# A planner without filler matmuls in a recurrent scan, and two block products laid four abreast

## The chip, the cores and the metric

The program runs on one core of one Trainium2 chip. The metric is the time of one execution on the device in microseconds (us); of the kernel before, three runs gave a median of 3036.94 us (3034.74 to 3039.24).

## What is computed

The model is a two-layer backbone of width 1024 over 1024 latent tokens, with 256 context tokens ahead of them. Layer 0 mixes tokens by a recurrence with 16 heads of 64 channels, once forwards and once backwards; layer 1 mixes by a Fourier transform; behind each stands a squared-ReLU MLP of hidden width 4096. Cut to what matters here:

```python
w_log = -softplus(-(w0[d] + tanh(xw @ w1[d]) @ w2[d])) - 0.5          # rates of the recurrence, per direction
decay = exp(-exp(w_log)); iclr = sigmoid(a0[d] + (xa @ a1[d]) @ a2[d])
k_d = k * (1 + (iclr - 1) * ka); a, b = -kk, kk * iclr                 # kk is k, normalised per head
def step(s, inp):                                                      # one token; s is (head, 64, 64)
    w_t, k_t, v_t, a_t, b_t = inp[:5]
    sa = einsum('bhvk,bhk->bhv', s, a_t)
    s = s * w_t[:, :, None, :] + sa[..., None] * b_t[:, :, None, :] + v_t[..., None] * k_t[:, :, None, :]
    y = einsum('bhvk,bhk->bhv', s, inp[5])
    return s, y
for d in range(2):                                                     # forwards and backwards
    yc, s_ctx = scan(context tokens, s0, reverse=d == 1)
    yl, _ = scan(latent tokens, s_ctx, reverse=d == 1)
x = x + ga1 * (readout(yl of both directions) @ wo)
x = x + ga2 * mlp(modulate(rmsnorm(x)))                                # layer 0
x = x + ga1 * (real(fft2 of modulate(rmsnorm(x))) @ ft_wo)             # layer 1
x = x + ga2 * mlp(modulate(rmsnorm(x)))
return rmsnorm(x) * final_g
```

All of it is in 32-bit floating point.

## The kernel before, in words

The program has four stages. The first computes the norms, the projections and the factors of the recurrence and writes these factors to HBM. The second is the scan. The third reads the scan's output back and runs the readout, and the last, the longest, is the MLP, the Fourier layer and the second MLP.

**The scan** treats 64 tokens (a chunk) at a time, so there are 20 steps: 4 over the context and 16 over the latent tokens. A step works on one chunk of each direction, d = 0 and d = 1, for 16 heads in pairs: a tile has heads on its partitions 0 to 63 and 64 to 127 (hh = 0 and 1) and 8 such pairs along its free axis (q, or y = 8 d + q over both directions). The matmuls of a step, with the line at which the profile books them, are:

- L951 (`mms`): products of the factors inside a chunk, four bursts of 8 matmuls. ScalarE (L960, L964) and VectorE (L967, L972) take them out of PSUM.
- L1130 (`turn`): transposes of the factors, two bursts.
- The inverse of a 64x64 triangular matrix per head and direction, `scan_invert`. The 64 rows are two blocks of 32. VectorE inverts the 16x16 diagonal blocks by a long series of small operations (L1071 to L1117), L1141 and L1154 (each two bursts of 32 matmuls) finish the two 32x32 diagonal blocks, and the block off the diagonal is a product of three: L1173 (`v_mm`), then a copy to SBUF, then L1184 (`g_mm`), then a copy into the inverse `tt`.
- L1008 (`x_mm`), L1017 (`u_mm`, which multiplies by `tt`) and L1031 (`s_mm`): the recurrence itself, each once per direction. The state of step i enters `x_mm` of step i + 1. L1047 and L1053 (`r_mm`, `y_mm`) make the output of latent steps.

The off-diagonal block joins the first half of a chunk with the second. The partitions are four groups of 32 (g = 0 to 3), and both directions keep the first half in groups 0 and 2 and the second in 1 and 3. So `v_mm` reads group 0 and writes group 1, or reads 2 and writes 3, alternating for 16 values of y; `g_mm` goes back the other way.

**The order of the work** is made by a planner (`Plan`). Every operation is added with its engine, a planned length in us and the data that it needs; `emit` then simulates all engines by these lengths, picks at each turn the operation that can start first (of equals the one with the longest chain behind it), and writes the program in that order. Each engine runs its queue in that order, so an operation whose inputs come late holds up all behind it on its engine. The planner also models TensorE's clock: time is cut in windows of 3.413 us (`TICK`), and work in a window is planned at half speed where the one before had too little of it; each operation has a `load`, the weight with which its time counts.

**Fills.** Where the planner sees TensorE idle ahead of an operation that opens a new PSUM bank, it writes dummy 128x128 matmuls of the identity into that bank, one per 0.218 us of the gap (`FILL`). They are L1843 in the profile. They stand in TensorE's queue like any other work.

The trace has two rows for each matmul of the scan (a 32-bit matmul is done in two passes) and as many weight loads; the transposes of L1130 have one.

## Time and profile before

| | |
|---|---|
| median of three runs | 3036.94 us |
| the profiled execution: its time, its span | 3052.24 us, 3050.2 us |
| its granted TensorE clock, mean | 0.947 |
| TensorE busy over the span | 2858.6 us, 94% |
| VectorE, ScalarE, GpSimd busy | 1880.4, 1014.3, 487.8 us |
| first and last L1843 rows of the scan in the trace | at 659.13 and 1254.96 us |

A profile's engines are PE (TensorE's matmuls), PEld (its weight loads), DVE (VectorE), ACT (ScalarE), POOL (GpSimd) and SP (the queue of the sync engine, which issues DMAs). A row of a group of instructions gives line, engine, operation, output<-input, the count after x, then busy us, mean ns of one, and the idle time of the engine just before them with what ended it. "issue" is time in which the engine waited for nothing that the profile shows.

### The profile page before, as it was taken

The numbers are of one execution on the slowest core, as the hardware profiler recorded it, in microseconds if no ns is written. First come the engines' busy times: TensorE is split into PE (matmuls) and PEld (weight loads), VectorE is DVE, ScalarE is ACT, GpSimd is POOL, SyncE is SP. The second block draws the span as 40 slices with busy tenths as digits, with TensorE's granted clock in tenths as the row PEclk, the third lists the DMA queues.
The fourth block names the chain that finished last, engine by engine and source line by source line (L and its number), as shares of the span: only waits on it lengthen the run. The fifth ranks groups of instructions, "written<-read, shape, count | busy, mean of one in ns | idle before, by whom it ended". The sixth has DMA issues, their size and how long they took to land.

```text
span 3050.2 us, 63412 instructions
## 1 busy us (share of the span) xinstructions
PE 2858.6 (94%) x26844; PEld 2225.1 (73%) x26844; DVE 1880.4 (62%) x3363; ACT 1014.3 (33%) x1974; POOL 487.8 (16%) x415
## 2 busy tenths in 40 slices
PE   9999989988887888799999999999899999999998
PEld 5443446467777777688788888887798788888887
DVE  5398695546667666787655665454876554454455
ACT  4263454345555555333212111112322111111121
POOL 2063453300000000111110111010421110111110
PEclk9999999968789897799999999999899999999999
DMA  9266475623345443643222322211121111111111
GB/s 280 83 180 185 129 195 172 181 83 101 113 125 154 124 124 120 205 132 97 90 86 90 111 90 90 63 62 34 47 76 42 56 49 49 42 56 49 35 45 56
DMA packets 297293, 312.90 MB, mean 103 GB/s; under 512 B 81025, under 2 KB 212225, under 8 KB 297009
## 3 DMA queue, kind: packets, MB, share of 16 engines
q1 hardware_dynamic: 295648, 304.01, 33.3%
q8 instruction: 210, 3.44, 0.5%
q0 software_dynamic: 1360, 4.84, 0.5%
q14 instruction: 75, 0.61, 0.1%
HBM read 246.38 MB, written 62.39 MB: 101 GB/s over the span
## 4 chain that ended last, share of the span: by engine, by line
PE 78%; DVE 10%; DMA 4%; issue 4%; ACT 3%; SPq 1%; POOL 1%; DVEq 0%; ACTq 0%; POOLq 0%
PE ps L368 17%; PE ps L370 17%; PE ps L369 17%; PE ps L624 6%; PE ps L621 4%; PE ps L951 3%; PE ps L1843 2%; DVE bU L460 1%; PE ps L1008 1%; PE ps L1031 1%; PE ps L1017 1%; PE ps L1154 1%; PE ps L578 1%; PE ps L1053 1%; PE ps L1141 1%
## 5 line engine op out<-in xcount | busy, mean ns | idle before, releaser
L368 PE MATMUL ps<-rU,rU 128*128 128x512 f32 (+3 forms) x2632 | 980.1, 372 | 16.8 <-DVE rX L1538 8.0
L370 PE MATMUL ps<-rU,rU 128*128 128x512 f32 (+3 forms) x2632 | 976.1, 371 | 6.2 <-DVE rU L1268 3.5
L369 PE MATMUL ps<-rU,rU 128*128 128x512 f32 (+3 forms) x2632 | 975.9, 371 | 0.1
L368 PEld LDWEIGHTS ps<-rU,rU 128*128 128x128 f32 x2632 | 501.5, 191 | 111.9 <-DVE rX L1538 8.9
L370 PEld LDWEIGHTS ps<-rU,rU 128*128 128x128 f32 x2632 | 501.5, 191 | 97.8 <-DVE rU L1268 4.8
L369 PEld LDWEIGHTS ps<-rU,rU 128*128 128x128 f32 x2632 | 501.9, 191 | 90.3 <-DVE rU L1352 0.4
L1538 DVE SCALAR_TENSOR_TENSOR rX<-ps,mods,rX 128x512 f32<-128x512 f32 (+1 forms) x528 | 375.6, 729 | 123.8 <-PE ps L370 121.7
L1517 ACT ACTIVATE rS<-ps 128x512 f32<-128x512 f32 x122 | 73.0, 598 | 681.5 <-PE ps L370 680.8
L1268 POOL TENSOR_TENSOR rU<-rW,rU 128x512 fp32r<-128x512 f32 x73 | 118.0, 1621 | 1001.6 <-PE ps L370 518.3
L624 PE MATMUL ps<-bU,bU 128*128 128x512 f32 (+1 forms) x544 | 235.1, 568 | 2.6 <-ACT bS L427 1.9
L427 ACT CAST rU<-rW 128x512 fp32r<-128x512 f32 x161 | 97.2, 617 | 349.0 <-PE ps L370 260.9
L1268 DVE TENSOR_TENSOR rU<-rW,rU 128x512 fp32r<-128x512 f32 x201 | 173.3, 881 | 25.4 <-ACT rU L427 25.3
L427 DVE CAST rU<-rS 128x512 fp32r<-128x512 f32 (+1 forms) x97 | 45.0, 469 | 232.8 <-ACT rS L1520 205.4
L427 DVE CAST rU<-rW 128x512 fp32r<-128x512 f32 x115 | 55.1, 491 | 212.6 <-PE ps L369 210.3
L624 PEld LDWEIGHTS ps<-bU,bU 128*128 128x128 f32 x544 | 99.5, 191 | 108.2 <-issue 96.3
L621 PE MATMUL ps<-bU,bU 128*128 128x512 f32 x304 | 140.9, 604 | 0.0
L951 PE MATMUL ps<-sU,sX 64*128 64x128 f32 (+1 forms) x1280 | 119.3, 338 | 17.5 <-DVE sU L967 5.9
L951 PEld LDWEIGHTS ps<-sU,sX 64*128 64x128 f32 x1280 | 105.7, 241 | 24.7 <-issue 6.6
L427 ACT COPY sU<-ps 32x512 f32<-32x512 f32 (+1 forms) x167 | 96.2, 577 | 79.6 <-PE ps L1154 27.6
L967 DVE TENSOR_TENSOR sU<-ps,sW 64x256 f32<-64x256 f32 x160 | 67.5, 422 | 70.7 <-ACT sX L960 39.1
L1268 POOL TENSOR_TENSOR rU<-rS,rU 128x512 fp32r<-128x512 f32 x41 | 64.1, 1566 | 289.8 <-ACT rU L427 154.8
L1843 PE MATMUL ps<-ident 128*128 128x128 f32 x664 | 98.9, 308 | 2.8 <-DMA ident<-in_k_ident_dram 2.6
(275 smaller groups left out, 3740.8 us busy)
## 6 DMA issues: line engine op xcount, KB each, us to landing
rW<-in_mlp_w_dram SPq DMA_DIRECT2D x256, 256.0 KB
rW<-in_k_mwt_dram SPq DMA_DIRECT2D x96, 256.0 KB
sX<-s_bk SPq DMA_DIRECT2D x40, 512.0 KB
s_ar<-bU SPq DMA_DIRECT2D x32, 512.0 KB
sU<-s_ar SPq DMA_DIRECT2D x64, 256.0 KB
sW<-in_k_mwt_dram SPq DMA_DIRECT2D x64, 256.0 KB
bU<-in_rk_wk_dram SPq DMA_DIRECT2D x48, 256.0 KB
bU<-in_rk_wv_dram SPq DMA_DIRECT2D x48, 256.0 KB
```

Of the source, the lines that this page charges most:

```text
L368: nc.tensor.matmul(out, w[0], x[0], start=start, stop=False)
L369: nc.tensor.matmul(out, w[0], x[1], start=False, stop=False)
L370: nc.tensor.matmul(out, w[1], x[0], start=False, stop=stop)
L427: self.nc.scalar.copy(out, src) if e == "act" else self.engines[e].tensor_copy(out, src)
L621: fn = lambda B=B, x=x, w=w, ms=ms, kt=kt: nc.tensor.matmul(B.tile, x[:, ms], w, start=kt == 0, stop=kt == KT - 1)
L624: fn = lambda B=B, x=x, w=w, ms=ms, kt=kt, n=n: nc.tensor.matmul(B.tile[:, :n], w[:, ms], x[:, :n], start=kt == 0, stop=kt == KT - 1)
L951: nc.tensor.matmul(BB[hh].tile[:, j * P : j * P + nr], bk[HR[hh], q, :], L[hh][HR[hh], q, :nr], start=True, stop=True)
L967: plan.add("dve", 0.41, lambda bv=bv, ro=ro, hh=hh, q4=q4, d=d, L=L: nc.vector.tensor_tensor(L[hh][ro, q4, 0:C], bv()[ro, :, 0:C], self.ma ...
L1268: plan.flex({"dve": n / 960 + 0.07, "pool": n / 440 + 0.08}, lambda e: self.engines[e].tensor_tensor(out(1), src(), f32(out(0)), ALU.subtr ...
L1517: plan.flex({"act": 0.53, "dve": 0.6}, lambda e, B=B, s=s: nc.scalar.activation(s.tile[:, :512], B.tile, AF.Relu) if e == "act" else nc.ve ...
L1538: plan.add("dve", n / 960 + 0.12, lambda B=B, m=m, n=n, xs=xs: nc.vector.scalar_tensor_tensor(xs(), B.tile[:, :n], self.mod(layer, 5, m), ...
L1843: self.plan.fill = lambda t: nc.tensor.matmul(t[:, :P], self.ident, self.ident, start=True, stop=True)
```

## The change

There are three parts.

**No fills from scan step 4 on.** A flag `bare` on an operation stops the planner from writing fills ahead of it. It is set for steps 4 to 19 and cleared for what comes after the scan.

**Planned lengths.** The planned lengths of the scan's matmul bursts are set to other values: most grow (0.95 to 1.1 or 1.15 us), `turn` shrinks (0.85 to 0.75). Nothing but the planner reads them, so they show only as another order.

**Halves swapped in direction 1.** For d = 1, the two 32-token halves of a chunk trade places on the partitions: two of the factor products of the first stage write their result with the halves exchanged (`hv(...)[:, :, flip]`), the masks are rolled by 32 accordingly, and the zero blocks of `tt` and the copies into `mab` follow. The first half of d = 0 then lies in groups 0 and 2, that of d = 1 in groups 1 and 3. `v_mm` now takes for each of 8 values of q four products, 0 to 1, 1 to 0, 2 to 3 and 3 to 2, all four groups at a time. The number of matmuls is the same, 32 in each burst. The result of `v_mm` has 128 partitions and 256 columns and is copied at once, where two copies of 32 partitions and 512 columns stood; that of `g_mm` is copied by four copies of 32x256 in place of two of 32x512. `g_mm` now needs all four copies of the diagonal blocks.

```diff
-        self.step, self.rank = None, 0.0
+        self.step, self.rank, self.bare = None, 0.0, False
...
-                  hold=hold, dear=self.dear, weigh=self.weigh)
+                  hold=hold, dear=self.dear, weigh=self.weigh, bare=self.bare)
...
             if e == "pe" and blank:
-                fills = max(0, int((start - since - self.SLACK) / self.FILL))
+                fills = 0 if op["bare"] else max(0, int((start - since - self.SLACK) / self.FILL))
                 for _ in range(fills):
                     since = self.clock(since, self.FILL, 1.0)
                 start = max(start, since)
...
-        self.flex_tt(n, bk[:, :ng, 0], gv(ta), p1[:, :ng], ALU.mult, [kta, kp1], [(kbk, 0)])
+
+        hv = lambda ap: ap.rearrange("p g (w t) -> p g w t", w=2)
+        self.flex_tt(n, hv(bk[:, :ng, 0])[:, :, flip], hv(gv(ta)), hv(p1[:, :ng]), ALU.mult, [kta, kp1], [(kbk, 0)])
         self.flex_tt(n, bk[:, :ng, 1, flip], gv(kd), p1[:, :ng], ALU.mult, [kkd, kp1], [(kbk, 1)])
-        self.flex_tt(n, ar[:, :ng, 0], gr(kk), p0[:, :ng, 0:C], ALU.mult, [kkk, kp0], [(kar, 0)])
+        self.flex_tt(n, hv(ar[:, :ng, 0])[:, :, flip], hv(gr(kk)), hv(p0[:, :ng, 0:C]), ALU.mult, [kkk, kp0], [(kar, 0)])
...
-            for g in (1, 3):
-                plan.add("pool", 0.6, lambda tt=tt, g=g: nc.gpsimd.memset(tt[32 * g : 32 * g + 32, :, 0:32], 0.0), (), [(("tt", j), g)])
+            for g in range(4):
+                d = 1 - g % 2
+                plan.add("pool", 0.4, lambda tt=tt, g=g, d=d: nc.gpsimd.memset(
+                    tt[32 * g : 32 * g + 32, 8 * d : 8 * d + 8, 32 * d : 32 * d + 32], 0.0), (), [(("tt", j), g)])
...
         for i in range(NCH):
             self.plan.step = i
+            self.plan.bare = i >= 4
             self.scan_step(i)
...
-        RZ = [[slice(hh * 64 + 32 * z, hh * 64 + 32 * z + 32) for hh in range(2)] for z in range(2)]
+
+        RZ = [[[slice(hh * 64 + 32 * (d ^ z), hh * 64 + 32 * (d ^ z) + 32) for hh in range(2)] for d in range(2)] for z in range(2)]
...
-                plan.add("pe", 0.95, mms, [kb, (kL, "a", 0), (kL, "a", 1)],
+                plan.add("pe", 1.15, mms, [kb, (kL, "a", 0), (kL, "a", 1)],
...
                     plan.add("act", 0.38, lambda B=B, hh=hh, ys=ys, d=d: nc.scalar.activation(
-                        mab[RZ[0][hh], :, ys].rearrange("p w q t -> p q w t"),
-                        B.tile[RZ[0][hh]].rearrange("p (q w t) -> p q w t", q=4, w=4)[:, :, 0:2], AF.Copy, scale=-0.5),
+                        mab[RZ[0][d][hh], :, ys].rearrange("p w q t -> p q w t"),
+                        B.tile[RZ[0][d][hh]].rearrange("p (q w t) -> p q w t", q=4, w=4)[:, :, (slice(0, 2), slice(1, None, -1))[d]], AF.Copy, scale=-0.5),
                         [B], [(kM, d, hh, h4, 0)], B)
                     plan.add("act", 0.28, lambda bv=bv, hh=hh, ys=ys, d=d: nc.scalar.activation(
-                        mab[RZ[1][hh], 0, ys], bv()[RZ[1][hh], :, 32:C], AF.Copy, scale=-0.5),
+                        mab[RZ[1][d][hh], 0, ys], bv()[RZ[1][d][hh], :, 32 - 32 * d : C - 32 * d], AF.Copy, scale=-0.5),
...
-            self.at = plan.add("pe", 0.95, x_mm, lall + vall, [B], B, load=0.95)
+            self.at = plan.add("pe", 1.1, x_mm, lall + vall, [B], B, load=0.95)
...
-            plan.add("pe", 0.95, u_mm, [kx, *kT], [U], U, load=0.5)
+            plan.add("pe", 1.1, u_mm, [kx, *kT], [U], U, load=0.5)
...
-                plan.add("pe", 1.1, s_mm, vall + [(kt_, 0), (kt_, 1)], [B, kt0], B, load=0.78)
+                plan.add("pe", 1.2, s_mm, vall + [(kt_, 0), (kt_, 1)], [B, kt0], B, load=0.78)
...
-                plan.add("pe", 0.95, r_mm, vall + [E["ks"], (kL, "a", 0), (kL, "a", 1)], [Y], Y, load=0.5)
-                plan.add("pe", 1.05, y_mm, vall + [(k2, hh, h4) for hh in range(2) for h4 in range(2)], [Y], Y, load=1.0)
+                plan.add("pe", 1.15, r_mm, vall + [E["ks"], (kL, "a", 0), (kL, "a", 1)], [Y], Y, load=0.5)
+                plan.add("pe", 1.15, y_mm, vall + [(k2, hh, h4) for hh in range(2) for h4 in range(2)], [Y], Y, load=1.0)
...
-            plan.add("pe", 0.85, turn, [S[d]["kb"]], [*TB[d]], load=0.5)
+            plan.add("pe", 0.75, turn, [S[d]["kb"]], [*TB[d]], load=0.5)
...
-            plan.add("pe", 0.7, lambda w=w: h_mm(w), [kxt, *ms], [(H, w)], load=0.15)
+            plan.add("pe", 0.85, lambda w=w: h_mm(w), [kxt, *ms], [(H, w)], load=0.15)
...
-            plan.add("pe", 0.75, lambda w=w: t_mm(w), [khp, kxd], [(T, w)], load=0.3)
+            plan.add("pe", 0.85, lambda w=w: t_mm(w), [khp, kxd], [(T, w)], load=0.3)
...
+
+        four = [(d, 2 * hh + d, 2 * hh + 1 - d) for hh in range(2) for d in range(2)]
+        own = lambda g: slice(32 * (g % 2), 32 * (g % 2) + 32)
+
         def v_mm():
-            for y in range(16):
-                for g in (0, 2):
-                    nc.tensor.matmul(V.tile[Q[g + 1], y * 32 : y * 32 + 32], mab[Q[g], 1, y, :], tr[Q[g], y, :], start=True, stop=True)
-
-        plan.add("pe", 0.75, v_mm, [ktr, *offs], [V], V, load=0.15)
+            for q in range(8):
+                for d, f, l in four:
+                    nc.tensor.matmul(V.tile[Q[l], q * 32 : q * 32 + 32], mab[Q[f], 1, 8 * d + q, :], tr[Q[f], 8 * d + q, :], start=True, stop=True)
+
+        plan.add("pe", 0.65, v_mm, [ktr, *offs], [V], V, load=0.25)
         vt, kvt = slot("vt")
-        for g in (1, 3):
-            plan.flex({"act": 0.58, "dve": 0.69}, lambda e, g=g: self.copy_on(e, vt[Q[g]].rearrange("p y t -> p (y t)"), V.tile[Q[g]]),
-                      [V], [(kvt, g)], V)
+        plan.flex({"act": 0.38, "dve": 0.42}, lambda e: self.copy_on(e, vt.rearrange("p q t -> p (q t)"), V.tile[:, :256]), [V], [kvt], V)
 
         def g_mm():
-            for y in range(16):
-                for g in (1, 3):
-                    nc.tensor.matmul(G.tile[Q[g - 1], y * 32 : y * 32 + 32], vt[Q[g], y, :], tt[Q[g], y, 32:64], start=True, stop=True)
-
-        plan.add("pe", 0.75, g_mm, [(kvt, 1), (kvt, 3), (kT, 1), (kT, 3)], [G], G, load=0.15)
-        for g in (0, 2):
-            plan.flex({"act": 0.58, "dve": 0.69}, lambda e, g=g: self.copy_on(
-                e, tt[Q[g], :, 32:64], G.tile[Q[g]].rearrange("p (y t) -> p y t", y=16)), [G], [(kT, g, "o")], G)
-        return tt, [(kT, g) for g in range(4)] + [(kT, g, "o") for g in (0, 2)]
+            for q in range(8):
+                for d, f, l in four:
+                    nc.tensor.matmul(G.tile[Q[f], q * 32 : q * 32 + 32], vt[Q[l], q, :], tt[Q[l], 8 * d + q, own(l)], start=True, stop=True)
+
+        plan.add("pe", 0.65, g_mm, [kvt, *[(kT, g) for g in range(4)]], [G], G, load=0.25)
+        for d, f, l in four:
+            plan.flex({"act": 0.38, "dve": 0.42}, lambda e, d=d, f=f, l=l: self.copy_on(
+                e, tt[Q[f], 8 * d : 8 * d + 8, own(l)], G.tile[Q[f], :256].rearrange("p (q t) -> p q t", q=8)), [G], [(kT, f, "o")], G)
+        return tt, [(kT, g) for g in range(4)] + [(kT, g, "o") for g in range(4)]
...
-        plan.dear, plan.weigh = REST_DEAR, REST_WEIGH
+        plan.dear, plan.weigh, plan.bare = REST_DEAR, REST_WEIGH, False
...
-        mask[b, 1, hh] = np.concatenate([-0.5 * strict, -0.5 * incl[:, ::-1]], 1)
-        mask[k, 1, hh] = np.concatenate([strict[::-1], incl[::-1, ::-1]], 1)
+        mask[b, 1, hh] = np.roll(np.concatenate([-0.5 * strict, -0.5 * incl[:, ::-1]], 1), 32, axis=0)
+        mask[k, 1, hh] = np.concatenate([np.roll(strict[::-1], 32, axis=1), incl[::-1, ::-1]], 1)
```

How the program's order moves, at three places. The first is TensorE's queue in scan step 12, from the last of `x_mm` to the first of the next chunk's products; L1184 before is L1192 now (`g_mm`), L1017 is L1023 (`u_mm`), L1008 is L1014. Before:

```order
L1008 MATMUL ps_95<-sU_188,sU_199 64x64
L1008 MATMUL ps_95<-sU_188,sU_198 64x64
L1184 MATMUL ps_94<-sU_173,sX_202 32x32 x32
L1843 MATMUL ps_96<-ident 128x128 x7
L1017 MATMUL ps_96<-sS_163,sU_173 64x64 x16
L951 MATMUL ps_91<-sU_191,sX_203 128x128
L951 MATMUL ps_90<-sU_190,sX_203 128x128
```

Now, at the same place:

```order
L1014 MATMUL ps_95<-sU_188,sU_199 64x64
L1014 MATMUL ps_95<-sU_188,sU_198 64x64
L1192 MATMUL ps_94<-sU_173,sX_202 32x32 x32
L1023 MATMUL ps_97<-sS_163,sU_173 64x64 x16
L1023 MATMUL ps_95<-sW_154,sU_173 64x64 x16
L957 MATMUL ps_91<-sU_191,sX_203 128x128
L957 MATMUL ps_92<-sU_190,sX_203 128x128
```

The seven fills between `g_mm` and `u_mm` are gone and nothing has been put in their place; the second `u_mm` has moved ahead of the next chunk's products. In the scan 115 fills stood before; 7 are left, all in the context steps.

The second place is ScalarE's queue in the same step, from the copy of `v_mm`'s result (sX from bank 94) to those of `g_mm`'s (sU_173 from bank 94). Before:

```order
L427 COPY sX_202<-ps_94 32x512 x2
L960 ACTIVATE sX_202<-ps_93 32x4x2x32
L960 ACTIVATE sX_202<-ps_92 32x4x2x32
L427 COPY sS_163<-ps_96 128x512
L427 COPY sW_154<-ps_95 128x512
L427 COPY sU_173<-ps_94 32x16x32 x2
```

Now:

```order
L427 COPY sX_202<-ps_94 128x256
L970 ACTIVATE sX_202<-ps_91 32x128
L970 ACTIVATE sX_202<-ps_92 32x128
L427 COPY sS_163<-ps_97 128x512
L970 ACTIVATE sX_202<-ps_93 32x128
L970 ACTIVATE sX_202<-ps_90 32x128
L427 COPY sW_154<-ps_95 128x512
L427 COPY sU_173<-ps_94 32x8x32 x2
```

One shorter copy stands where two stood, and two of the four copies of `g_mm`'s result are on ScalarE, the others on VectorE.

The third is VectorE's queue at the end of the inverse of the last step, 19, from the transposes ahead of L1141 to the one behind L1154 (STREAM_TRANSPOSE from bank 94); L893, now L898, is a product of the modulation weights, 128x512 rows that a DMA brings (`mod_part`). Before:

```order
L1117 STREAM_TRANSPOSE sU_175<-sU_175 128x512
L427 COPY sU_189<-sU_170 64x512
L1309 SCALAR_TENSOR_TENSOR rW_12529<-rM_12799,rW_12529 128x512
L893 SCALAR_TENSOR_TENSOR sW_157,sF_207<-sW_157,sF_205 128x512
L1146 SCALAR_TENSOR_TENSOR sU_174<-ps_94,sS_160 128x16x16
L1312 TENSOR_REDUCE rM_12799<-rW_12672 128x8
L893 SCALAR_TENSOR_TENSOR sW_156,sF_207<-sW_156,sF_205 128x512
L1315 RECIPROCAL rM_12799<-rM_12799 128x8
L893 SCALAR_TENSOR_TENSOR sW_159,sF_207<-sW_159,sF_205 128x512
L1166 STREAM_TRANSPOSE sX_202<-ps_94 128x512
```

Now:

```order
L1043 TENSOR_TENSOR sU_171<-ps_96,sU_170 128x512
L427 COPY sU_187<-sU_170 64x512
L1152 SCALAR_TENSOR_TENSOR sU_174<-ps_94,sS_160 128x16x16
L1316 TENSOR_REDUCE rM_12791<-rW_12345 128x8
L898 SCALAR_TENSOR_TENSOR sW_159,sF_207<-sW_159,sF_205 128x512
L999 TENSOR_TENSOR sU_170<-sU_171,pcs 128x512
L1317 SCALAR_TENSOR_TENSOR rW_12345<-rM_12791,rW_12345 128x512
L1172 STREAM_TRANSPOSE sX_202<-ps_94 128x512
```

Between the first matmuls of the inverse and the transpose of its last part, three modulation products stood ahead of the transpose; now one does.

More of the change, by code (lines that the diff above doesn't have):

```diff
@@ L278 @@
 SCAN_RINGS = (
-    ("bk", (8, P), *_row(4, "X0", 0, 1024)), ("mab", (2, 16, 32), *_row(3, "X1", 0, 1024)), ("tr", (16, 32), ("X1", 3072)), ("vt", (16, 32), ("X1", 3584)),
+    ("bk", (8, P), *_row(4, "X0", 0, 1024)), ("mab", (2, 16, 32), *_row(3, "X1", 0, 1024)), ("tr", (16, 32), ("X1", 3072)), ("vt", (8, 32), ("X1", 3584)),
     *[(f"L{h}", (8, P), *[(f"U{2 * j + h}", 0) for j in range(6)]) for h in range(2)],
```

## The prediction

> **What bounds the kernel now.** The change touches the scan, so the first question is where that lies and what it waits for. The page's engine line and two of its slice rows come first.
>
> ```profile
> PE 2858.6 (94%) x26844; PEld 2225.1 (73%) x26844; DVE 1880.4 (62%) x3363; ACT 1014.3 (33%) x1974; POOL 487.8 (16%) x415
> PE   9999989988887888799999999999899999999998
> PEclk9999999968789897799999999999899999999999
> ```
>
> The slices are 76 us each. TensorE is full nearly everywhere; the dip in its busy time and clock, in slices 9 to 17, is the scan. The view by stretches gives its start, its steady part and its end: length, busy us (rows) of each engine, granted clock, DMA.
>
> ```profile
> 600.00:690.00 90.00, 79.32 (x1056) 60.86 (x1054) 40.27 (x97) 38.00 (x90) 5.06 (x10) 0.72 0.32 96
> 690.00:1230.00 540.00, 452.82 (x14035) 418.46 (x14035) 375.22 (x907) 310.83 (x660) 11.55 (x19) 0.86 0.42 124
> 1230.00:1300.00 70.00, 48.14 (x856) 46.34 (x855) 47.01 (x98) 25.34 (x47) 9.03 (x7) 0.76 0.66 216
> ```
>
> In the steady part TensorE is busy 453 of 540 us, VectorE 375. Next, what TensorE's other 87 us wait for in those 540 us: total, times, longest.
>
> ```profile
> PE ps L1154 <- issue: 18.5, 14, 2.3
> PE ps L1031 <- issue: 13.3, 7, 4.4
> PE ps L1053 <- issue: 8.6, 4, 2.4
> PE ps L1173 <- DVE sU L427: 5.0, 2, 3.6
> PE ps L1008 <- issue: 4.7, 4, 1.9
> PE ps L951 <- issue: 4.5, 3, 2.4
> PE ps L1184 <- ACT sX L427: 4.2, 5, 1.3
> PE ps L1141 <- issue: 3.5, 6, 1.6
> ```
>
> The "issue" rows make 53 of the 87 us: no data is missing then. What is, the timeline of TensorE shows (start, length, line, rows; in brackets the idle time ahead).
>
> ```profile
> 857.52 0.46 PE L1031 MATMUL ps<-sU,sU 128*64 128x64 f32 x9 [1.14 <-issue]
> 857.91 1.16 PE L951 MATMUL ps<-sU,sX 64*128 64x128 f32 x16
> 858.90 0.66 PE L1130 MATMUL ps<-ident,sX 64*128 64x64 f32 x16
> 859.49 0.94 PE L1154 MATMUL ps<-sU,sU 32*32 32x32 f32 x87
> 860.98 0.56 PE L1154 MATMUL ps<-sU,sU 32*32 32x32 f32 x41 [0.55 <-issue]
> 861.47 1.15 PE L1053 MATMUL ps<-sU,sU 128*64 128x64 f32 x32
> 862.45 1.10 PE L1008 MATMUL ps<-sU,sU 128*64 128x64 f32 x32
> 863.48 0.71 PE L1130 MATMUL ps<-ident,sX 64*128 64x64 f32 x16
> 864.12 0.45 PE L1008 MATMUL ps<-sU,sU 128*64 128x64 f32 x6
> 865.04 1.03 PE L1008 MATMUL ps<-sU,sU 128*64 128x64 f32 x26 [0.47 <-issue]
> ```
>
> From one stall to the next there are 9+16+16+87 = 128 matmuls, then 41+32+32+16+6 = 127: with the weight load of each, blocks of 256 instructions. The blocks begin at 857.52, 860.98 and 865.04, so 3.5 to 4.1 us apart. I read this as the instructions' own delivery, a block at a time; bursts of small matmuls eat a block faster than the next one comes. The steady part has 28,070 instructions, 110 blocks; at 4.06 us each they would take 447 of the 540 us. So two things carry the scan: TensorE's time (453 us, with 53 us of such stalls it is 506 of 540), and close below it the delivery, which takes back part of what TensorE gains.
>
> **The change part by part.** The groups that carry the terms, from the scan (600 to 1270 us):
>
> ```profile
> L1843 PE MATMUL ps<-ident 128*128 128x128 f32 x230 | 38.8, 324 | 0.0
> L1154 PE MATMUL ps<-sU,sU 32*32 32x32 f32 x2560 | 35.8, 212 | 19.4 <-issue 19.4
> L1173 PE MATMUL ps<-sX 32*32 32x32 f32 x1280 | 28.5, 206 | 19.2 <-ACT sU L427 14.2 <-DVE sU L427 5.0
> L1184 PE MATMUL ps<-sU,sX 32*32 32x32 f32 x1280 | 28.2, 203 | 10.5 <-ACT sX L427 5.7 <-DVE sX L427 3.6 <-issue 1.1
> L960 ACT ACTIVATE sX<-ps 32x256 f32<-32x256 f32 x160 | 59.7, 373 | 79.6 <-PE ps L951 70.6 <-DVE sU L967 6.5
> L427 ACT COPY sX<-ps 32x512 f32<-32x512 f32 x34 | 19.6, 577 | 14.6 <-PE ps L1173 12.9 <-DVE sX L427 1.4
> ```
>
> *Fills.* 108 of the scan's 115 go: 216 of the 230 rows, 38.8 x 216/230 = 36.4 us of TensorE's queue. That is the upper end. The lower end is nothing, where the operation behind the fills had to wait for its data anyway. Two places show both:
>
> ```profile
> 906.28 3.78 PE L1843 MATMUL ps<-ident 128*128 128x128 f32 x16
> 907.00 0.69 DVE L427 COPY sU<-ps 32x512 f32<-32x512 f32 x1 [0.83 <-ACT sU L427]
> 909.99 1.21 PE L1017 MATMUL ps<-sW,sU 64*64 64x64 f32 x34
> 1031.57 1.83 PE L1843 MATMUL ps<-ident 128*128 128x128 f32 x14
> 1031.69 1.17 ACT L427 COPY sU<-ps 32x512 f32<-32x512 f32 x2
> 1033.33 1.15 PE L1017 MATMUL ps<-sS,sU 64*64 64x64 f32 x32
> ```
>
> L1017 waits for the copies of the inverse. At 906 the last one ends at 907.69 and L1017 starts at 909.99: of 3.78 us of fills 2.3 are lost. At 1031 the copies end at 1032.86 and L1017 starts at 1033.33: of 1.83 us 0.5 are lost. Together 2.8 of 5.6 us; as the second kind, a gap filled to within half a microsecond, is what the planner means to make, I take 40%: **-14 us**.
>
> *Four abreast.* L1173 and L1184 have the shape of L1154, 32x32 by 32x32, and together as many rows, 2560; they run two products abreast, L1154 four. 2560 rows cost 56.7 us the one way and 35.8 the other. Upper end: 56.7 - 35.8 = 20.9 us. Lower end: L1154 pays 19.4 us of issue stalls for its speed, L1184 1.1; were they to come with the speed, 1.5 us would be left. L1154 takes two bursts in a row, 256 instructions, while `v_mm` and `g_mm` are 128 each with other work between, so it is not the worst case: **-12 us**.
>
> All four products write one PSUM bank, in four groups of partitions. The Trainium skill, TensorEngine Tiling (Array Packing), section "Gotcha 1: PSUM Pressure", says "Different row tiles cannot access same PSUM bank simultaneously"; by that this term would be nothing. L1154 does write one bank from four row groups and costs 0.63 of what two abreast cost (35.8 of 56.7), so the trace speaks against the rule here; it stays as a small rival.
>
> *Copies.* `g_mm` waited 5.7 + 3.6 us in all for the copies of `v_mm`'s result (L1184's row). Two of 0.577 us become one of 256 columns; the nearest row is L960, 0.373 us. The four copies behind `g_mm` have that length too, two per engine, 0.75 us where one or two of 0.577 stood: no gain. Ends 0 and -9.3 us; I take **-4**.
>
> *Clock.* A window of 3.41 us at half speed costs 1.7 us of TensorE work. The scan already has such windows with TensorE busy throughout:
>
> ```profile
> 692.15:695.56 3.41, 3.41 (x94) 0.50 0.22 87
> ```
>
> In the order, the 100 fills of steps 4 to 19 stand in 21 blocks. If every block kept one window at full speed, 21 x 1.7 = 36 us are lost; if none, nothing. Most blocks are short like the one at 1031, and work moves up into their place: I take three windows, **+5 us**.
>
> *Order and planned lengths.* They cost nothing by themselves. The scan's end holds the largest single wait, the modulation rows that VectorE needs ahead of the last inverse:
>
> ```profile
> 1235.39 11.35 DMA sW<-in_k_mwt_dram
> ```
>
> Three such products stood there ahead of the transpose, now one (the third place of the order); but the loads also follow one another otherwise on SP's queue, behind writes of the scan's output that wait for it. Between -11 and +11 us; I take 0, as one profiled wait does not say which load will be late.
>
> *First stage, masks, zero blocks, a wider wait.* In the first stage two products per factor keep their element counts and gain an axis in the pattern; the row is that of such products on the slower engine.
>
> ```profile
> L460 POOL TENSOR_TENSOR bU<-bX,bS 128x512 f32<-128x512 f32 (+1 forms) x39 | 54.3, 1395 | 32.4 <-DMA s_ar<-bU 23.3 <-ACT pcs L825 3.8 <-issue 2.6
> ```
>
> TensorE, at 8 to 9 tenths in the first eight slices, hides that; without it, 96 products (48 factors) that got a tenth slower would add 13 us of engine time over two engines, 7 us at most. Four memsets more fall to POOL, which is busy 11.55 of 540 us. `g_mm` now waits for all four copies of the diagonal blocks; they are queued ahead of `v_mm`'s copy, and behind `g_mm` stands `u_mm`, which needs all four in any case. I count nothing for these.
>
> Sum: -14 - 12 - 4 + 5 = **-25 us**. The profiled execution took 3052.24 us (span 3050.2, 2 us around it), so 3027. It lies 0.5% above the median of the runs; in their terms 3036.94 - 25 = **3012 us**.
>
> **The rivals.** All in terms of the median.
>
> *The delivery takes it back.* Blocks of 256 set the pace wherever TensorE gets faster. For it: 53 us of issue stalls, and a fill is four instructions in 0.34 us (two rows of 38.8/230), slow work that gave the delivery time. Against it: 447 us of blocks in 540. The price: 108 fills are 432 instructions, 1.7 blocks, 7 us; the products give the 1.5 us of the lower end: -8, **3029 us**. The Trainium skill, Runtime: NRT & Kernel Launch, section "Instruction fetch mechanics", tells of 16 KiB blocks of 256 instructions and calls the cost of crossing into one "mostly hidden"; by that this rival would have no chance. The block's size is that of the trace, the hiding isn't: 53 us.
>
> *One bank, no overlap.* The page's rule holds for `v_mm` and `g_mm`: -25 + 12 = -13, **3024 us**.
>
> *The clock stays down (slower).* Place: steps 4 to 19. With fills gone, windows hold less dense work and the half-speed share rises. Clock 0.86 means 28% of the time at half speed. For it: the start, 600 to 690, at 0.72. At half of the time, 0.22 x 540 / 2 x 0.84 (busy share) = +50 us against gains of 30: +20, **3057 us**. It decides from 18 windows more (30 / 1.7). Against it: the windows of 692 dropped while TensorE was busy, so fills of idle time are not what holds the clock alone.
>
> *The full price.* Fills at 60% (-22), 20.9, 9.3, and half of the wait at the end (-6), clock +5: -53, **2984 us**.
>
> **How the numbers follow.** Forecast 0.47 (its own range 2997 to 3027, half of the three gains more or less); delivery 0.18; one bank 0.03; clock 0.20; full price 0.12. Within 0.2% means 3031 to 3043; that is about what a measurement of this kernel can tell. Of each case the part that falls there, faster: 0.45 + 0.10 + 0.02 + 0.12 = 0.69 (forecast, delivery, one bank, full price); the same: 0.02 + 0.08 + 0.01, and 0.04 for the mild end of the clock's, 0.15; slower: the rest of the clock's, 0.16. The range, 2984 to 3050, leaves out half of the last rival and half of the clock's.
>
> **What would show it.** In the changed kernel's profile: L1183 and L1192 (the two products) near 18 us each in place of 28.5 and 28.2 (the bank rule: unchanged); L1851 with some 14 rows in the scan; issue stalls in the scan's steady part at 53 to 70 us (the delivery rival: 85 or more); clock there between 0.83 and 0.88 (the clock rival: below 0.78); waits of TensorE for copies and VectorE up by some 20 us, where the harmless fills stood. The forecast fails if the clock falls, or if the stretch from 690 us to the readout does not shrink by about 25 us while those rows come out as said: then the bound was the chain through VectorE and not TensorE's time.

## The result and the profile after

The change took 3014.26 us, the median of four runs (3011.36 to 3018.24), against 3035.84 us before (3026.54 to 3039.24): a ratio of 0.9925, with an interval of 0.99 to 0.9949. That is 22 us less; 25 were forecast. Measured again with the first experiments it was 0.9913 (0.99 to 0.9926), 27 us. The total is right, but two of its terms, the fills and the order, are not, as the experiments show.

The profile after, its engine line, two slice rows and the three stretches that the prediction used:

```profile
PE 2820.9 (94%) x26640; PEld 2187.5 (73%) x26640; DVE 1883.4 (62%) x3380; ACT 997.1 (33%) x1971; POOL 496.4 (16%) x425
PE   9999989988878878899999999999899999999998
PEclk9999989978888888899999999999799999999999
600.00:690.00 90.00, 79.55 (x1033) 58.89 (x1031) 39.02 (x97) 38.40 (x93) 5.95 (x12) 0.73 0.33 98
690.00:1230.00 540.00, 431.40 (x14367) 396.47 (x14366) 397.63 (x978) 307.25 (x679) 14.60 (x26) 0.85 0.46 135
1230.00:1300.00 70.00, 58.85 (x559) 56.75 (x558) 58.52 (x96) 25.57 (x51) 18.47 (x14) 0.93 0.65 210
```

TensorE is busy 431 of 540 us in the steady part in place of 453, and more of the program fits into them. The groups of the products (600 to 1270 us), and then what TensorE waits for from 690 to 1230 us (total, times, longest):

```profile
L1192 PE MATMUL ps<-sU,sX 32*32 32x32 f32 x1280 | 17.3, 200 | 8.0 <-ACT sX L427 4.6 <-issue 3.3
L1183 PE MATMUL ps<-sX 32*32 32x32 f32 x1280 | 16.4, 198 | 12.3 <-ACT sU L427 5.7 <-DVE sU L427 2.2 <-DVE sU L973 2.2
```

```profile
PE ps L1160 <- issue: 18.4, 13, 4.2
PE ps L1037 <- issue: 11.9, 7, 3.4
PE ps L1147 <- issue: 10.0, 9, 2.2
PE ps L1023 <- ACT sU L427: 7.4, 11, 2.8
PE ps L1059 <- issue: 5.9, 4, 2.1
PE ps L1183 <- ACT sU L427: 5.7, 6, 1.7
```

The products went from 56.7 to 33.7 us, and of fills 14 rows are left in the scan. All issue rows of the view make 60.1 us, the copies (L427) appear among the waits.

**Where the time went.** The first profile of before (3052 us) was a long one, so it was profiled a second time.

> A second profile of the kernel before, unchanged. Its first one (3052 us) is longer than 40 of the 42 runs of it so far, whose median is 3041; there the scan, from the first step's first x_mm to L368, took 633.9 us, and the first stage up to that x_mm 638.5, which is the shortest seen in any profile here (638 to 653). Theory 'the first profile's scan was a long one': this one shows a scan of 620 to 626 us, so that fills left out (617.6 and 622.8 in two profiles) change nothing, as their time says (ratio 1.0008). Rival: the scan is 630 to 637 us again; then leaving out the fills takes 11 to 16 us off the scan and something outside it gives them back.

That run took 3042.14 us, its scan 622.0 us: the theory came true, the first profile's scan had been 12 us longer. The stretches are read from TensorE's timeline. Of the kernel before, profiled again: the first x_mm of steps 0 and 4, the last g_mm of steps 18 and 19, the readout's first product.

```profile
643.96 1.33 PE L1008 MATMUL ps<-sU,sU 128*64 128x64 f32 x20
769.15 1.47 PE L1008 MATMUL ps<-sU,sU 128*64 128x64 f32 x32
1209.69 0.72 PE L1184 MATMUL ps<-sU,sX 32*32 32x32 f32 x33 [0.63 <-issue]
1246.21 1.92 PE L1184 MATMUL ps<-sU,sX 32*32 32x32 f32 x64 [1.26 <-ACT sX L427]
1265.95 0.58 PE L368 MATMUL ps<-rU,rU 128*128 128x256 f32 x1 [7.54 <-ACT rU L427]
```

The same five places of the change:

```profile
642.90 1.33 PE L1014 MATMUL ps<-sU,sU 128*64 128x64 f32 x20
770.00 1.21 PE L1014 MATMUL ps<-sU,sU 128*64 128x64 f32 x34
1191.33 0.75 PE L1192 MATMUL ps<-sU,sX 32*32 32x32 f32 x64
1218.77 0.80 PE L1192 MATMUL ps<-sU,sX 32*32 32x32 f32 x64
1238.69 0.58 PE L368 MATMUL ps<-rU,rU 128*128 128x256 f32 x1 [4.51 <-ACT rU L427]
```

| stretch, us | before, again | change, two profiles | difference | forecast |
|---|---|---|---|---|
| to step 0's x_mm | 644.0 | 642.9, 637.8 | -3.6 | 0 |
| steps 0 to 3 | 125.2 | 127.1, 130.1 | +3.4 | 0 |
| steady: step 4's x_mm to the end of step 18's g_mm | 441.3 | 422.1, 425.2 | -17.6 | -25 |
| last inverse: to the end of step 19's g_mm | 37.7 | 27.5, 28.2 | -9.9 | 0 (±11) |
| to L368 | 17.8 | 19.1, 17.0 | +0.2 | 0 |
| rest | 1774.4 | 1777.8, 1775.5 | +2.2 | 0 |

The second profile of the change is of the run just below. In the first profile of before the stretches were 638.5, 127.6, 449.6, 39.3, 17.4 and 1777.7 us, so the steady part of one kernel differed by 8 us between two profiles. That is the grain of this table, and of every steady stretch below that rests on one profile.

### The profile page after: what moved, and what is told of

The parts are those of the page before. It is cut to its first block, busy times and chain, and to the rows that moved or that the text cites. A ratio compares the mean times of both kernels' runs of the same rounds, so it can differ in the third digit from the quotient of the medians.

```text
span 3016.5 us, 63005 instructions
## 1 busy us (share of the span) xinstructions
PE 2820.9 (94%) x26640; PEld 2187.5 (73%) x26640; DVE 1883.4 (62%) x3380; ACT 997.1 (33%) x1971; POOL 496.4 (16%) x425
## 4 chain that ended last, share of the span: by engine, by line
PE 70%; DVE 11%; issue 4%; DMA 3%; ACT 3%; POOL 0%; SPq 0%; DVEq 0%; ACTq 0%; POOLq 0%
PE ps L368 17%; PE ps L370 17%; PE ps L369 17%; PE ps L621 4%; PE ps L624 3%; PE ps L957 2%; PE ps L1037 1%; PE ps L1059 1%; PE ps L1023 1%; DVE bU L460 1%; PE ps L1160 1%; PE ps L1014 1%; DVE rU L1276 1%; PE ps L1147 1%; DVE bS L803 1%
## 5 line engine op out<-in xcount | busy, mean ns | idle before, releaser
L368 PE MATMUL ps<-rU,rU 128*128 128x512 f32 (+3 forms) x2632 | 979.9, 372 | 13.6 <-DVE rX L1546 8.0
L368 PEld LDWEIGHTS ps<-rU,rU 128*128 128x128 f32 x2632 | 501.9, 191 | 107.5 <-DVE rX L1546 8.8
L427 ACT CAST rU<-rW 128x512 fp32r<-128x512 f32 x161 | 97.2, 616 | 351.9 <-PE ps L370 255.6
L427 DVE CAST rU<-rW 128x512 fp32r<-128x512 f32 x115 | 55.2, 490 | 215.9 <-PE ps L369 210.0
L427 DVE CAST rU<-rS 128x512 fp32r<-128x512 f32 (+1 forms) x97 | 45.0, 469 | 226.2 <-ACT rS L1528 198.9
L624 PEld LDWEIGHTS ps<-bU,bU 128*128 128x128 f32 x544 | 100.5, 193 | 107.5 <-issue 98.0
L427 ACT COPY sU<-ps 32x512 f32<-32x512 f32 (+2 forms) x186 | 96.0, 517 | 75.6 <-PE ps L1160 33.0
L621 PEld LDWEIGHTS ps<-bU,bU 128*128 128x128 f32 x304 | 56.5, 192 | 61.2 <-issue 57.6
```

The costliest lines, as they stand in the source:

```text
L368: nc.tensor.matmul(out, w[0], x[0], start=start, stop=False)
L427: self.nc.scalar.copy(out, src) if e == "act" else self.engines[e].tensor_copy(out, src)
L621: fn = lambda B=B, x=x, w=w, ms=ms, kt=kt: nc.tensor.matmul(B.tile, x[:, ms], w, start=kt == 0, stop=kt == KT - 1)
L624: fn = lambda B=B, x=x, w=w, ms=ms, kt=kt, n=n: nc.tensor.matmul(B.tile[:, :n], w[:, ms], x[:, :n], start=kt == 0, stop=kt == KT - 1)
```

## The experiments

**Each part in a fixed order.** Three kernels keep the order of before or of the change and alter only whether fills are issued, or how the 32 products within a burst follow one another; the change itself ran beside them.

> The changed kernel once more, as the mark for the runs beside it. In its profile the readout's first product (L368) starts 33.8 us earlier than in the profile of before (1238.7 against 1272.5), and what follows is as long as before (1778 us in both). Of the 33.8 us, the stretch from the fifth step's first product x_mm to the twentieth's gives 18.3 (461.1 to 442.8), and the stretch from there to L368, the scan's end, 19.4 (45.2 to 25.8); the steps before lose 4. Theory 'TensorE's time' expects the steady stretch to repeat within 5 us, and the time near 3014 us. If the scan's end is a matter of luck of one execution (a late load), it comes out elsewhere between 26 and 45 us; if it is the order of the loads, it stays within 5 us of 26.

It repeated: 3014.79 us (3013.73 to 3015.58), with 24.0 us for the scan's end by the mark of that text and 446.4 for its steady stretch. So the short end is the order's and no accident. The mark that I used there for the scan's end, step 19's x_mm, stands elsewhere in each order, so the table above takes g_mm in its place; the 19 us that the mark gave to the end are 10.

*Fills not issued, old order.* The flag `bare` is set as in the change, but read only where the program is written:

```diff
-                for _ in range(op["fills"][0]):
+                for _ in range(0 if op["bare"] else op["fills"][0]):
```

> The kernel before, planned as before, but the 100 fills that stand in steps 4 to 19 are not issued: the order on every engine is that of before. Theory 'TensorE's time' (prediction's term): -14 us in the steady stretch, the scan's end still near 45 us, so about 3022. By the share that the steady stretch returned in the change (18 of 59 us of TensorE time taken out): 33 us of fills give -10 us. Rival 'order': what the change brought is the new order of loads and steps, so fills alone give 0 (+-3 us), 3036. Rival 'clock': without fills the granted clock of the steady part falls below 0.80 and the time rises above 3040.

3044.18 us (3033.01 to 3054.84), ratio 1.0008 (0.9996 to 1.0021): nothing gained. The steady stretch was 436.8 us. The view by stretches tells why; the first two rows are those of before again, the others those of this run, each time the window used so far and then the steady stretch itself.

```profile
690.00:1230.00 540.00, 453.36 (x14311) 419.75 (x14314) 380.86 (x920) 315.75 (x670) 11.10 (x19) 0.87 0.43 127
769.15:1210.41 441.26, 372.41 (x11602) 345.39 (x11602) 313.45 (x778) 261.51 (x555) 8.38 (x15) 0.87 0.43 129
```

```profile
690.00:1230.00 540.00, 428.39 (x14028) 396.06 (x14018) 375.72 (x909) 312.55 (x660) 12.13 (x20) 0.86 0.43 129
763.82:1200.65 436.83, 352.00 (x11431) 325.81 (x11425) 312.52 (x773) 260.69 (x555) 8.38 (x15) 0.87 0.44 130
```

In the steady stretch TensorE was busy for 372 us and idle for 69 in before again, for 352 and 85 in this run: of 20 us less work, 16 came back as waits. A second profile of this kernel (below, under the clock) has 359 and 83: 13 us less work, 14 more of waits. In both, the waits for data (all rows but issue) rose from 22 us to 35. The fills of the old order stand in gaps.

*Fills back, new order.* The count is taken as before, without moving the planner's clock, and 52 fills are issued in steps 4 to 19.

```diff
-                fills = 0 if op["bare"] else max(0, int((start - since - self.SLACK) / self.FILL))
-                for _ in range(fills):
+                fills = max(0, int((start - since - self.SLACK) / self.FILL))
+                for _ in range(0 if op["bare"] else fills):
```

> The changed kernel in its own order, with 52 fills issued again where the new plan leaves TensorE gaps (half as many as before's 100, some 17 us of TensorE time). Theory 'TensorE's time': +5 to +7 us beside the changed kernel, all of it in the steady stretch; the scan's end stays at 26. Rival 'order': 0 (+-3 us). Rival 'clock': the fills pay for themselves, granted clock 0.87 or more in place of 0.85 and the time 5 us shorter.

3022.7 us, ratio 0.9941 (0.9926 to 0.9956): 9 us more than the change (2 to 15 by both intervals). The steady stretch was 432.8 us, 9.1 over the change's mean of 423.7. Here fills cost time: their group grew by 104 rows and 18.6 us (600 to 1230 us), and half of that was paid. It is not simply their length that was added. In the steady stretch TensorE's busy time rose by only 4 us (342 against 339 and 338), the waits for data fell from 36 us to 30, and the issue stalls rose from 47 and 50 us to 60. Why they rose stays open.

*Two abreast, new order.*

```diff
-            for q in range(8):
-                for d, f, l in four:
+            for d, f, l, q in two:    # the 16 products of d = 0, then the 16 of d = 1
```

> The changed kernel in its own order and with the same number of instructions, but v_mm and g_mm issue first the 16 products of one direction and then those of the other, so that two go side by side in place of four. Theory 'TensorE's time' (prediction's term): their two groups go back from 33.7 to about 57 us, and the time rises by 12 us, at most 23. Rival 'delivery': the slower products give the instruction delivery time, the stalls put down to issue in the steady part fall from 60 to below 45 us, and the time rises by 1.5 to 5 us only. Rival 'order': 0 (+-3 us), since the order is kept.

3028.03 us, ratio 0.9958 (0.9944 to 0.9972): 14 us more than the change (8 to 19). In its groups (600 to 1270 us) the two products cost 51.3 us:

```profile
L1191 PE MATMUL ps<-sU,sX 32*32 32x32 f32 x1280 | 26.3, 204 | 5.2 <-ACT sX L427 3.5 <-issue 1.7
L1183 PE MATMUL ps<-sX 32*32 32x32 f32 x1280 | 25.0, 201 | 9.8 <-ACT sU L427 3.1 <-DVE sU L427 2.3 <-issue 2.2
```

The steady stretch was 434.0 us, 10.3 longer. TensorE was busy for 349 us of it and idle for 85; in the change's two profiles for 339 and 338, and idle for 83 and 87. The gain there is all TensorE time, and no wait took it back. The whole scan was longer by less, 602.4 us against 595.8 and 600.5, as the stretches on both sides of the steady one came out 2 to 5 us shorter; the profiled execution was also the shortest of its six, so most of the 14 us are seen in the time alone. The delivery rival, which wanted fewer stalls with slower products, is refuted: issue rows sum to 66.9 us here and in the change beside it.

**The parts, each planned anew.** Now the edits are left in or out as the diff has them, and the planner makes another order for each.

> The kernel before with the nine new planned lengths alone (278 fills in the program in place of 332, two products abreast as before). In the new plan the last modulation product stands 0.8 us ahead of step 20's x_mm; before it stood 14.8 us behind. Theory 'the end is set by these rows': the end falls from 45 to 26 (+-5) us; the steady stretch has some 50 fills less, 0 to -7 us: -19 to -26 us, ratio 0.992 to 0.994. Rival 'the end belongs to the other parts': the end stays at 45, ratio 0.998 to 1.000.

3046.77 us, ratio 1.001 (0.9995 to 1.0025). The last inverse did shrink, from 37.7 to 29.3 us, but the steady stretch grew from 441.3 to 453.6 (in the first profile of before it was 449.6). My -19 to -26 us failed.

> The kernel before with the rule 'no fills from step 4 on' alone, and planned anew with it. Prediction's term: -14 us, ratio 0.9955. By the run that kept the old order and left out the fills: 0, ratio 1.000 (+-0.0015). Rival 'order': planned anew, with the last modulation product 29.5 us behind step 20's x_mm, the scan's end grows to 55 us or more and the time rises above 3048, ratio over 1.002.

3067.29 us, ratio 1.0093 (1.0061 to 1.0125): 28 us slower than before, more than any of the three expectations. The steady stretch grew to 459.5 us, the last inverse shrank to 32.5: rival 'order' had the sign, but not the place, as the loss is not at the scan's end.

> The changed kernel with the nine planned lengths of before (the two of the products stay with them): no fills in steps 4 to 19, four abreast, another order. Prediction's term: the lengths are worth 0, so 3014 (+-4), ratio 0.990 to 0.993. Rival 'order': they carry a good part of the gain, and without them the time is 3022 or more, ratio over 0.994; the scan is then over 604 us in place of 596 to 600.

3050.14 us, ratio 1.003 (1.0016 to 1.0044): slower than before, and 36 us (30 to 41) slower than the change, although the products are as in the change and steps 4 to 19 have no fills either (steps 0 to 3 have 48 here and 7 in the change, and took 124.1 us, no more than there). Rival 'order' came true, the prediction's term did not. The steady stretch took 458.8 us. The view by stretches, of the window used so far and of the steady stretch itself, then the latter of the change:

```profile
690.00:1230.00 540.00, 417.43 (x13669) 383.99 (x13666) 383.72 (x942) 288.88 (x642) 12.67 (x22) 0.83 0.43 126
766.29:1225.05 458.76, 350.31 (x11350) 322.43 (x11347) 325.99 (x814) 243.95 (x543) 11.23 (x19) 0.82 0.45 130
```

```profile
770.00:1192.08 422.08, 338.60 (x11268) 311.74 (x11268) 315.69 (x795) 239.22 (x534) 10.63 (x20) 0.85 0.47 138
```

TensorE is busy 417 us of 540, the least of all runs, and the steady part is nearly the longest. In its steady stretch it is busy for 350 us and idle for 108, in the change's for 339 and 83: 12 us more of busy time, which is what nearly the same work takes at the lower granted clock (339 x 0.85 / 0.82 = 351), and 25 more of waits. Most of what the waits gained is issue stalls, 65 us against 47 and 50 in the change's two profiles; the waits for data are 43 us against 36.

> The changed kernel, but its planner places fills as before did (345 in the program in place of 230), and the order follows from that. In this plan the last modulation product stands 31.6 us behind step 20's x_mm; in the change 1.2 us ahead of it. Theory 'the end is set by these rows': the end goes from 26 back to 45 us or more, and the 115 fills cost what 52 cost twice, some 8 to 16 us: 3040 to 3050, ratio 1.000 (+-0.003). Rival 'only the fills count': +8 to +16 us beside the change, the end at 26, ratio 0.994 to 0.9965.

3037.41 us, ratio 0.9973 (0.9957 to 0.999): 18 us (12 to 24) slower than the change, so the fill rule matters beside the other two parts. Its plan put 55 fills in steps 4 to 19, but also 151 ahead of the readout's operations, where the change has 88. Its one profile fell on an execution with a mean clock of 0.907 (the other nine had 0.952 to 0.958), so its stretches are a rough guide only: its scan, 597.3 us, was no longer than the change's in spite of the fills and the clock, with a steady stretch of 414.4, and the rest took 1791.6. That speaks against a loss in the scan; how the 18 us divide stays open.

**The last inverse.** In before, VectorE stands behind the load of a modulation row; in the profile again too, in its chain of waits:

```profile
1228.45 11.38 DMA sW<-in_k_mwt_dram
```

One kernel writes those loads and their products earlier in the order from step 8 on and leaves TensorE, ScalarE and GpSimd as they were:

```diff
+                    new[op["n"]] = min(new[op["n"]], x if op["eng"] == "q" else max(x, *(new[p] + 8.0 for p in op["pre"] if ops[p]["eng"] == "q")))
+            order.sort(key=lambda z: (new[z[1]], z[0]))
```

> The kernel before, with its order on TensorE, ScalarE and GpSimd kept; only the loads of the modulation rows (L893's operands) and their products on VectorE are written earlier in the order from step 8 on, as early as their four buffers allow, so that the last four stand in step 18 in place of behind step 19's first products. Theory 'the scan's end is set by these rows': the wait of 11.35 us for in_k_mwt at 1235 goes, the stretch from step 20's x_mm to L368 falls from 45 to 30 (+-5) us, the steady stretch stays at 461 (+-6): -15 us, ratio 0.995. Rival 'the next late load takes its place' (in_rk_g, s_hg): the end stays above 40 us, ratio 1.000.

3048.89 us, ratio 1.0018 (1.0001 to 1.0036). The wait for the modulation row went, and the last inverse fell from 37.7 to 31.1 us, but the steady stretch rose to 454.2. In its chain a load of the readout now holds VectorE just as long:

```profile
1243.88 11.49 DMA rW<-s_v
```

So the rival came true, or nearly (by the mark of that text the end took 39.1 us). The change's own order has a shorter last inverse and no longer steady part, which moving these rows alone did not give. What the wait was worth shows on VectorE just ahead of the transpose behind the last inverse's L1154, in before again and in the change:

```profile
1239.86 0.69 DVE L893 SCALAR_TENSOR_TENSOR sW<-sW,sF 128x512 f32<-128x512 f32 x1 [7.47 <-DMA sW<-in_k_mwt_dram]
1240.48 0.71 DVE L1166 STREAM_TRANSPOSE sX<-ps 128x512 f32<-128x512 f32 x1
```

```profile
1212.95 0.72 DVE L1172 STREAM_TRANSPOSE sX<-ps 128x512 f32<-128x512 f32 x1 [1.56 <-PE ps L1160]
```

In before the transpose stands behind 7.5 us of idle time for the load; in the change it waits only for its own matmul. So far as one wait of one profile can show it, that is 6 of the 9.9 us. It is no merit of one part: the four other plans made for the experiments above have a last inverse of 27.8 to 32.5 us as well.

**The clock.**

> A second profile of the kernel before with its fills not issued. Its twelve runs lay between 3033 and 3055 us, and the longer ones have the lower granted clock (0.955 at 3033, 0.941 at 3055); the profiled one was among the shortest (3035, 0.952). Theory 'clock': this profile, at 3040 to 3050 us with a mean clock near 0.947, shows the loss in the scan: granted clock of the steady part 0.83 or less in place of 0.86, the steady stretch 455 to 462 us in place of 447.5, and the readout as long as ever. Rival: the loss lies in the readout or in the first stage, and the steady stretch stays below 450.

3049.97 us, but the loss is not where I put it: the steady stretch took 442.1 us (436.8 in the other profile of this kernel), while the first stage took 650.8 in place of 638.6. The first 600 us, of the earlier profile and of this one:

```profile
0.00:600.00 600.00, 567.67 (x2033) 276.88 (x2034) 397.32 (x547) 270.02 (x511) 229.57 (x207) 0.97 0.62 175
```

```profile
0.00:600.00 600.00, 570.29 (x2012) 278.37 (x2012) 392.13 (x539) 266.77 (x506) 227.19 (x206) 0.95 0.60 171
```

It is one program, and the edit lies behind this stage. Of the 15 us between these two executions 12 lie there, so the rival came true and the clock reading of the scan falls; granted clock and time go together in the first stage, though two profiles do not show which is the cause.

Could the fills behind the scan go as well? This kernel keeps the change's order and issues none but the first stage's:

```diff
+                for _ in range(0 if op["step"] is not None else op["fills"][0]):
```

> The changed kernel in its own order, and none of the 178 fills behind the first stage issued: 7 in steps 0 to 3 and 171 behind the scan, where they take 44 us of TensorE time (16.8 of them between 1240 and 1300 us, where the readout waits for its loads). By the scan's old order, where 100 fills left out brought 0, the time stays at 3014 (+-3), ratio 0.991: the waits and the clock take it. By the scan's new order, where 52 fills (17 us of TensorE time) cost 8 us, half of 44 us comes out: 2992, ratio 0.984. Rival 'clock': between 1230 and 1500 us the granted clock falls from 0.93 to 0.97 to below 0.90, and the time rises by 5 us or more, ratio over 0.9925.

3022.36 us, ratio 0.9954 (0.9938 to 0.997): 12 us (6 to 19) slower than the change by the ratios, 8 by the medians. The scan was as short as ever (593.6 us), but the rest took 1780.6 us, 3 and 5 us more than in the change's two profiles. From 1230 to 1300 us, of the change beside the first experiments and of this run:

```profile
1230.00:1300.00 70.00, 61.21 (x582) 58.81 (x580) 58.97 (x99) 27.11 (x53) 18.82 (x15) 0.95 0.67 217
```

```profile
1230.00:1300.00 70.00, 45.28 (x411) 42.60 (x407) 58.46 (x96) 24.83 (x50) 17.73 (x14) 0.86 0.65 208
```

The granted clock falls from 0.95 to 0.86 there, and over the execution from 0.950 to 0.943 in these two profiles. The clock rival was right on the time. Its clock below 0.90 came only in this window; from 1230 to 1500 us it was 0.93, against 0.96 and 0.97 in the change. So the fills outside steps 4 to 19 pay for themselves, and that they do so by the clock is likely but not isolated.

The halves alone, in before's order or planned anew, were not tried, nor the copies by themselves.

## Why the prediction was right, and where it was not

**Four abreast: right.** The step took -12 us between 1.5 and 20.9. In a fixed order it measured 14 us by time (8 to 19) and 10.3 in the steady stretch; the two groups fell to 33.7 us, a little under the estimate of 35.8, and issue stalls came with it only in L1192's 3.3 us (4.3 in the change's second profile). All four row groups write one bank: the rule of the Trainium skill, TensorEngine Tiling (Array Packing), section "Gotcha 1: PSUM Pressure", that different row tiles cannot use a bank at the same time, would have left 57 us; 33.7 were measured. In the whole scan's profile the gain was smaller, 2 to 7 us, and only the times show the rest.

**Fills: the step failed.** "I take 40%" was one share for all fills, from two places. In before's order the share was nothing (-1 to +6 us where -14 was forecast): the TensorE time that was freed, 20 and 13 us in two profiles, came back as 16 and 14 us of waits. The place at 1031, where the gap was filled to half a microsecond, was the rule there, and that at 906 the exception. In the change's order 52 fills cost 9 us, half of their time. How much a fill costs is a property of the order that it stands in.

**Order and planned lengths: the step failed.** "They cost nothing by themselves", with ±11 us for the scan's end, was the worst of the terms. Given before's lengths, the change loses 36 us; the fill rule alone, in the order that it makes, costs 28; the lengths alone give 3 the wrong way, which is within the noise. Only the last inverse stayed within the bound: -9.9 us, where I took 0. The 0 came near for the change's own plan, but the step gives no reason why it should there and not in the other plans. That is luck.

**Clock: not settled.** Between 690 and 1230 us the granted clock was 0.86 and 0.87 in two profiles of before, 0.85 in both of the change, and 0.86 in the run without any fills behind the first stage, whose steady part is the change's. Taken as 0.02, the fall would be 4% more of 540 us at half speed, 6 windows of 3.41 us where 3 made the +5; but two profiles of one program differ by 0.01, so neither sign nor size is shown.

**Copies: not settled.** L1192's wait for the copies fell from 9.3 us to 4.6 and 2.8 in the change's two profiles, 5 to 7 against a forecast of 4, but no run isolates it.

**What bounds the scan: half right.** TensorE's time counts, as the two-abreast run shows without a loss. But it does not carry the scan by itself: with the old lengths TensorE was busy for 350 us of the steady stretch in place of 372 in before again, and the stretch was 17.5 us longer. The prediction saw that data waits would rise where harmless fills stood (some 20 us; the steady stretch shows 22 before and 36 after) and that the delivery lies close below. It did not see that both kinds of waits are set anew with each plan.

**The sum.** The forecast for the steady part was -25 us, the measured change -17.6 against before again; the two profiles of before leave it anywhere from there to -26. If the prices found in the change's order add up, the 52 fills (9) and the products (10) make the -17.6, with 2 the other way for the rest of the order, the copies and the clock together; no run took both out at once. The last inverse's -9.9, taken as 0, filled the gap, and steps 0 to 3 (+3.4) took some back. So by this reading the total came out partly because two errors cancelled, which is luck.

**The rivals.** Delivery: between 690 and 1230 us issue stalls rose from 55.4 to 60.1 and 66.9 us, inside the 53 to 70 named and far from 85; in the steady stretch itself they were 46 us in before again, 47 and 50 in the change. So the delivery did not take the gain back. That it comes in blocks is borne out: from one such stall of over 0.3 us to the next, TensorE's rows in that window come to a multiple of 128, give or take 4, in 33 of 36 cases before and 41 of 45 in the change. The Trainium skill's "mostly hidden" (Runtime: NRT & Kernel Launch, section "Instruction fetch mechanics") does not describe these 60 us. Clock down: not in the change, yet it is part of what happened with the old lengths (0.82 in the steady stretch) and, at another place, without the fills of the readout (0.86). One bank: no, by the two-abreast run. Full price: no.

## What to carry to other kernels

Where a planner writes the order, an edit of its inputs has two effects, the one that is meant and a new order; here the second was worth up to 36 us, more than any part. Measure a part with the order frozen before giving it a price, and give a planned order's own effect a wide range in place of nothing. Profile more than one execution before reading a stretch to a few us. Dummy work is neither free nor waste: what it costs depends on whether something else is late at that place, so test each stage apart.

## What had not been expected of the hardware

The same program's first stage took 638.6 us in one execution and 650.8 in another, with a granted clock of 0.97 and 0.95 over its first 600 us; over all profiles of these kernels it ran from 637.8 to 653.3 us. Single profiles of two kernels can so differ by as much as one part of the edit is worth.

Leaving out the fills outside steps 4 to 19 (171 of the 178 stand behind the scan) lowered the granted clock between 1230 and 1300 us from 0.93 and 0.95 to 0.86 and made the execution 8 to 12 us longer, while the scan's fills bought no clock beyond the spread between profiles: between 690 and 1230 us 0.86 and 0.87 with them, 0.86 and 0.85 without in one order, 0.86 with them and 0.85, 0.85 and 0.86 without in the other.

How long TensorE stood in issue stalls depended on the order of nearly the same matmuls: from 43 us of the steady stretch, with the modulation rows moved in before's order, to 65, with the old planned lengths in the change.
